# A two-layer diffusion backbone: the up products of its four FFNs in seven block products, with the norm applied ahead of them

## The chip, the cores and the metric

The kernel runs on one core of one Trainium2 chip. The metric is the device time of an execution in microseconds. The kernel before takes 2856.15 us, the median of three runs (2855.18, 2856.15 and 2861.4 us).

## The reference: what is computed

Two layers work on 512 latent tokens and 256 context tokens, 1024 features each, in float32. A layer is a half-step FFN, a token mixer (a convolution, a gated linear attention and a softmax attention side by side between one input and one output projection), and a second half-step FFN. The last FFN has latent tokens only.

```
def pre(x, mod, j, g):
    return rms_norm(x, g) * (1 + mod[:, :, 3 * j + 1]) + mod[:, :, 3 * j]

def half_ffn(x, mod, j, g, w1, w2):
    gu = pre(x, mod, j, g) @ w1          # w1: 1024 x 5632
    a, u = jnp.split(gu, 2, axis=-1)     # gate a and value u, 2816 columns each
    return x + 0.5 * mod[:, :, 3 * j + 2] * ((jax.nn.silu(a) * u) @ w2)
```

`mod` holds nine modulation vectors per layer and kind of token, `silu(c) @ w_ada[i] + b_ada[i]`, with `w_ada[i]` of 1024 x 9216 numbers (a matrix times two vectors: one for the latent tokens, one for the context).

## The kernel before, in words

**Layout.** Features lie on the partitions: the residual x is eight tiles `xt` (K tiles) of 128 features by 768 tokens, the latent ones first. An FFN has 22 column tiles of gate and 22 of value; f counts them, one of each. The four FFNs are called FFN1 to FFN4 here, in the order in which they run.

**Exact pairs.** A float32 operand is kept as a high part, rounded to the type fp32r, and the rest: `split` (L141 to L143) makes the high part on ScalarE (ACT) and the rest on VectorE (DVE). `mm3` (L386 to L393) multiplies two such pairs in three passes, hi by hi (L389), hi by lo (L391) and lo by hi (L393).

**Up.** For each f, `up` (L412 to L428) takes the gate tile and then the value tile. `load_split` (L131 to L139) fetches 512 KB of weights into one of two `raw` buffers and splits them into `whi` (ACT, L137) and `wlo` (DVE, L138), three buffers each. Then come eight K tiles by three passes by two chunks of tokens: 386 and 384 columns in FFN1 to FFN3, 256 and 258 in FFN4. `evac` multiplies the sum by 1/rms from PSUM (DVE, L465) and applies Silu or Identity (ACT, L468); gate and value are multiplied (DVE, L423) and split into `gh` and `gl` (L142, L143).

**The norm comes after.** `Scale.feed` (L355) writes x times the gain as a pair `sh`, `sl` (L362 on ACT, L363 on DVE), which needs no statistics, so that the first products can begin while squares are still being summed (L260 on ACT, L263 on GpSimd, POOL). Two more columns carry the shift vectors through the same products. In FFN1 a class `Head` starts the first tiles while the shifts are still being computed.

**Down.** Two f make a round. After the ups of a round come the down products of the round before, eight output tiles by 512 and 256 tokens; each is added to `xt` by DVE (`add_gated`, L399).

**The modulation vectors.** Vectors 0 and 1 of layer 0 are products on TensorE at the start. The other fourteen are filled in beside the FFNs by `ada` (L183): it loads 256 KB tiles `adaw`, ACT scales each by one number per partition (L195, one operation for each kind of token), DVE adds (L197), and one product per half with ones sums over the partitions (L206). An up is followed by 8 such steps in FFN1, 3 or 4 in FFN2 and FFN3, none in FFN4. The loads rotate through six slots of a group called d.

**What sets the order.** The program text gives the order, and each engine works through its own list; all loads are issued by one queue, SP, in that order too. A load that waits for its buffer holds up those behind it.

Some lines, of `up` and of `ada`:

```
            for t in (f, FT + f)[len(uv):]:
                w = load_split(w1_d[l, i, t])
                p = bigt("up")
                for k in range(KT):
                    mm_up([p[:, p0 + t0:p0 + t0 + n] for t0, n in cols], w, k, cols)
...
                r = slot(tags, "adaw", (P, 512))
                nc.sync.dma_start(out=r, in_=wada_d[l, m, k, :, half * 512:(half + 1) * 512])
                for v in range(nv):
                    t = acc[v] if k == 0 else slot("F", "adat", (P, 512))
                    nc.scalar.activation(out=t, in_=r, func=AF.Copy, scale=sc[:, k, v:v + 1])
                    if k:
                        nc.vector.tensor_tensor(out=acc[v], in0=acc[v], in1=t, op=ALU.add)
```

## Time and profile before

| | |
|---|---|
| runs (three) | 2855.18, 2856.15, 2861.4 us; median 2856.15 |
| profiled execution: span | 2857.3 us; nothing is reported outside the span |
| mean granted TensorE clock | 0.987 of full speed |
| TensorE (PE) busy | 2781.7 us, 97% |
| PE weight loads (PEld, beside PE) | 2541.2 us, 89% |
| DVE busy | 1768.5 us, 62% |
| ACT busy | 1200.8 us, 42% |
| POOL busy | 136.4 us, 5% |
| FFN1, FFN2, FFN3, FFN4 (from the first to the last of their products) | about 62 to 636, 1030 to 1590, 1592 to 2160, 2480 to 2857 us |

The table shares the span among engines that work side by side, so it says who is nearly always busy, and not what a piece of work costs. A matmul's own duration contains the filling and draining of the array, which the next one overlaps: what a matmul costs is the distance between the starts of two neighbours. Names such as `up<-sh,whi` are output and inputs, `128x386` is partitions by elements, x2 joins two like instructions.

### The profile page before, as it was taken

How to read it: one execution, taken by the hardware profiler on the slowest of the kernel's cores; microseconds unless marked ns; L12 is line 12 of the kernel's file. 1: busy time of each engine (PE TensorE's matmuls, PEld its weight loads, DVE VectorE, ACT ScalarE, POOL GpSimd, SP SyncE). 2: the span in 40 equal slices, each digit the busy share in tenths (PEclk: the TensorE clock that was granted, in tenths of full speed). 3: DMA queues.
4: the chain of work that ended last, by engine and by line, in shares of the span. 5: the costliest groups of instructions: out<-in, count | busy, mean ns of one | idle time of the engine just before them, and what ended most of it. 6: DMA issues, size and time to landing. Idle time of an engine off the chain costs nothing. (4 is left out here: it accounts for less than half of the span.)

```text
span 2857.3 us, 42932 instructions
## 1 busy us (share of the span) xinstructions
PE 2781.7 (97%) x17498; PEld 2541.2 (89%) x17498; DVE 1768.5 (62%) x2974; ACT 1200.8 (42%) x1908; POOL 136.4 (5%) x134
## 2 busy tenths in 40 slices
PE   8999999999899999999999999999999989999999
PEld 4999999988687899999999999999997768999998
DVE  4786874464897565566465746454546588555555
ACT  4665662233347454254252523232324447432322
POOL 1000000010300100000000100000001110100000
PEclk9999999999999999999999999999999999999999
DMA  7443441221211243233231313231312131222322
GB/s 255 144 144 129 141 130 60 67 93 58 65 43 27 86 139 101 82 118 107 78 118 56 116 66 111 74 119 60 98 57 84 47 88 28 91 89 95 98 97 89
DMA packets 98501, 267.67 MB, mean 94 GB/s; under 512 B 11520, under 2 KB 11904, under 8 KB 98304
## 3 DMA queue, kind: packets, MB, share of 16 engines
q1 hardware_dynamic: 98304, 264.93, 28.7%
q8 instruction: 137, 2.24, 0.3%
q14 instruction: 60, 0.49, 0.1%
HBM read 249.16 MB, written 7.34 MB: 90 GB/s over the span
## 5 line engine op out<-in xcount | busy, mean ns | idle before, releaser
L137 ACT CAST whi<-raw 128x1024 fp32r<-128x1024 f32 (+1 forms) x314 | 324.6, 1044 | 1110.8 <-PE up L391 524.2
L389 PE MATMUL up<-sh,whi 128*128 128x386 f32 (+1 forms) x2808 | 691.4, 327 | 2.2 <-ACT sh L362 1.2
L391 PE MATMUL up<-sl,whi 128*128 128x386 f32 (+1 forms) x2808 | 687.8, 325 | 4.7 <-DVE sl L363 4.7
L393 PE MATMUL up<-sh,wlo 128*128 128x386 f32 (+1 forms) x2808 | 686.0, 325 | 0.1
L465 DVE TENSOR_TENSOR upv<-up,rb 128x770 f32<-128x770 f32 (+2 forms) x177 | 157.2, 889 | 639.0 <-PE up L393 634.7
L389 PEld LDWEIGHTS up<-sh,whi 128*128 128x128 f32 x2808 | 493.1, 190 | 12.4 <-ACT whi L137 4.2
L391 PEld LDWEIGHTS up<-sl,whi 128*128 128x128 f32 x2808 | 495.9, 190 | 7.5 <-DVE sl L363 7.3
L393 PEld LDWEIGHTS up<-sh,wlo 128*128 128x128 f32 x2808 | 494.1, 190 | 2.1 <-DVE upv L465 1.7
L399 DVE SCALAR_TENSOR_TENSOR xt<-dn,mods,xt 128x512 f32<-128x512 f32 (+1 forms) x616 | 375.2, 632 | 123.0 <-PE dn L393 122.3
L389 PE MATMUL dn<-gh,whi 128*128 128x512 f32 (+1 forms) x1232 | 429.9, 349 | 3.3 <-DVE xt L399 3.2
L138 DVE TENSOR_TENSOR wlo<-raw,whi 128x1024 fp32r<-128x1024 f32 (+1 forms) x314 | 378.6, 1215 | 83.3 <-ACT whi L137 75.1
L391 PE MATMUL dn<-gl,whi 128*128 128x512 f32 (+1 forms) x1232 | 427.7, 347 | 0.0
L393 PE MATMUL dn<-gh,wlo 128*128 128x512 f32 (+1 forms) x1232 | 426.4, 347 | 0.0
L195 ACT ACTIVATE adat<-adaw,sc 128x512 f32<-128x512 f32 x392 | 258.9, 715 | 84.0 <-DVE adacc L197 76.7
L389 PEld LDWEIGHTS dn<-gh,whi 128*128 128x128 f32 x1232 | 232.8, 189 | 45.0 <-ACT whi L137 7.9
L393 PEld LDWEIGHTS dn<-gh,wlo 128*128 128x128 f32 x1232 | 232.9, 189 | 31.2
L391 PEld LDWEIGHTS dn<-gl,whi 128*128 128x128 f32 x1232 | 233.0, 189 | 29.5
L197 DVE TENSOR_TENSOR adacc<-adacc,adat 128x512 f32<-128x512 f32 x392 | 250.4, 684 | 7.9 <-ACT adat L195 6.3
L468 ACT ACTIVATE upv<-upv 128x512 f32<-128x512 f32 (+1 forms) x308 | 179.7, 625 | 33.8 <-DVE upv L465 33.6
L389 PE MATMUL pj<-nh,whi 128*128 128x512 f32 (+1 forms) x328 | 120.5, 371 | 8.5 <-DVE var L572 4.3
L263 POOL TENSOR_TENSOR acc<-acc,sq 128x512 f32<-128x512 f32 (+1 forms) x72 | 76.1, 1057 | 1075.1 <-ACT sq L260 1069.7
L391 PE MATMUL pj<-nl,whi 128*128 128x512 f32 (+1 forms) x328 | 120.9, 369 | 2.4 <-DVE nl L332 2.3
(216 smaller groups left out, 2798.7 us busy)
## 6 DMA issues: line engine op xcount, KB each, us to landing
raw<-in_w_dram SPq DMA_DIRECT2D x264, 512.0 KB, 3.5
adaw<-in_wada_dram SPq DMA_DIRECT2D x288, 256.0 KB, 3.3
raw<-in_wt_dram SPq DMA_DIRECT2D x26, 512.0 KB, 3.4
raw<-in_wo_dram SPq DMA_DIRECT2D x16, 512.0 KB, 3.6
raw<-in_wk_dram SPq DMA_DIRECT2D x8, 416.0 KB, 3.2
xt<-in_xT_dram SPq DMA_DIRECT2D x8, 384.0 KB, 7.9
park<-xt SPq DMA_DIRECT2D x8, 384.0 KB, 2.3
xt<-park SPq DMA_DIRECT2D x8, 384.0 KB, 5.2
```

The source lines that it names most:

```text
L137: nc.scalar.copy(out=hi[:, :n], in_=r[:, :n])
L138: nc.vector.tensor_tensor(out=lo[:, :n], in0=r[:, :n], in1=hi[:, :n].bitcast(F32), op=ALU.subtract)
L195: nc.scalar.activation(out=t, in_=r, func=AF.Copy, scale=sc[:, k, v:v + 1])
L197: nc.vector.tensor_tensor(out=acc[v], in0=acc[v], in1=t, op=ALU.add)
L263: eng.tensor_tensor(out=self.acc[:, t0:t0 + n], in0=self.acc[:, t0:t0 + n], in1=s[:, :n], op=ALU.add)
L389: nc.tensor.matmul(out=o, lhsT=w[0], rhs=m[0][:, t0:t0 + n], start=first, stop=False)
L391: nc.tensor.matmul(out=o, lhsT=w[0], rhs=m[1][:, t0:t0 + n], start=False, stop=False)
L393: nc.tensor.matmul(out=o, lhsT=w[1], rhs=m[0][:, t0:t0 + n], start=False, stop=last)
L399: nc.vector.scalar_tensor_tensor(out=x, in0=o[:, :n], scalar=mods[l][:, v, mod * KT + d:mod * KT + d + 1], in1=x, op0=ALU.mult, op1=ALU.add)
L465: nc.vector.tensor_tensor(out=a[:, t0:t0 + n], in0=p[:, c0:c0 + n], in1=rb[:, t0:t0 + n], op=ALU.mult)
L468: nc.scalar.activation(out=a[:, c], in_=a[:, c], func=AF.Silu if t == f else AF.Identity, bias=a[:, NX + v:NX + v + 1])
```

## The change

**Up products.** The eight K tiles are taken as two halves of four, the tokens as two halves (384 and 384, or 256 and 256 in FFN4), and gate and value of one f as the two blocks of columns. Of a 2 by 2 block product the seven-product form needs seven block products in place of eight: each is 4 K tiles by three passes by one half of the tokens. Its operands are sums and differences of blocks, of the weights (made by POOL in place in the raw tiles, L448 and L449, then split anew) and of the activations (made once per FFN by a class `Combos` in place of `Scale`, on DVE and POOL). The results are joined by sums on DVE and one on POOL (L484).

**The norm ahead of them.** `Combos` needs the finished 1/rms of a half of the tokens before it can make that half's operands. The first two of the seven products use the first half only: for f = 0 to 4 (`HEADS`) they are issued while the second half is being made, and these five gate tiles are loaded twice.

**What is moved with it.** Of the additions for the modulation vectors, DVE now scales and adds the latent one in a single operation (L187); ACT scales the tile in place for the other (L191) and POOL adds it (L193). The tiles `adaw` lie in two slots of group m in place of six of group d. Each half vector is summed and transposed on its own: 144 transposes in place of 72. Steps per up are 7, 5, 4 and 0. Down products come between the two ups of a round in place of behind both. Buffers: `raw` 3, `whi` and `wlo` 4, group E 9 slots. Shift columns, `Scale`, `Head` and the vector start under way are gone; the last round of FFN2 ends by halves of 384 tokens.

```diff
-SLOTS = {"a": 4, "b": 4, "c": 2, "d": 6, "A": 8, "E": 5, "F": 4, "v": 1, "q": 2, "m": 2}
+SLOTS = {"a": 4, "b": 4, "c": 2, "d": 6, "A": 8, "E": 9, "v": 1, "q": 2, "m": 2}
...
+HEADS = 5
+RAW = 3
+RING = 4
...
-                r = slot(tags, "adaw", (P, 512))
+                r = slot("m", "adaw", (P, 512))
                 nc.sync.dma_start(out=r, in_=wada_d[l, m, k, :, half * 512:(half + 1) * 512])
...
+                    nc.vector.scalar_tensor_tensor(out=acc[0], in0=r, scalar=sc[:, k, 0:1], in1=acc[0],
+                                                   op0=ALU.mult, op1=ALU.add)
+                if nv > 1:
+                    t = r if k else acc[1]
+                    nc.scalar.activation(out=t, in_=r, func=AF.Copy, scale=sc[:, k, 1:2])
                     if k:
-                        nc.vector.tensor_tensor(out=acc[v], in0=acc[v], in1=t, op=ALU.add)
+                        nc.gpsimd.tensor_tensor(out=acc[1], in0=acc[1], in1=t, op=ALU.add)
...
+        def build(self, h):
+            nh = self.nh
+            rb = self.spread(self.half(h))
+            yield
+            for p in range(4):
+                a = self.normed(p, h, rb)
+                if h == 0:
+                    self.h0.append(a)
+                    self.pair("xb", a, self.TAGS["b"], ("11", "21"))
+                else:
...
+                    nc.vector.tensor_tensor(out=t13[:, 0], in0=a[:, 0], in1=self.h0[p][:, 0], op=ALU.subtract)
+                    nc.gpsimd.tensor_tensor(out=t24[:, 0], in0=a[:, 1], in1=t13[:, 0], op=ALU.subtract)
+                    nc.vector.tensor_tensor(out=t13[:, 1], in0=a[:, 1], in1=a[:, 0], op=ALU.subtract)
+                    nc.gpsimd.tensor_tensor(out=t24[:, 1], in0=self.h0[p][:, 1], in1=t24[:, 0], op=ALU.subtract)
...
+                    split(b[:, 0], b[:, 1], a[:, 1])
...
+                    self.pair("xt", t13, self.TAGS["13"], ("T1", "T3"))
+                    self.pair("xt", t24, self.TAGS["24"], ("T2", "T4"))
...
+        def prod(o, w, c0, b, start, stop):
+            for p in range(4):
+                ws = slice(c0 + p * P, c0 + (p + 1) * P)
+                hi, lo = b[p]
+                nc.tensor.matmul(out=o, lhsT=w[0][:, ws], rhs=hi, start=start and p == 0, stop=False,
...
+        def up(f, e):
+            ra = load(w1_d[l, i, f])
+            ru = load(w1_d[l, i, FT + f])
+            w1 = wsplit(ra) if e is None else None
+            s1t = wp.tile([P, 512], F32, tag="s1t", name="s1t", bufs=1)
+            lo, hi = slice(0, 512), slice(512, 1024)
+            sub = lambda out, a, b: nc.gpsimd.tensor_tensor(out=out, in0=a, in1=b, op=ALU.subtract)
+            nc.gpsimd.tensor_tensor(out=s1t, in0=ru[:, lo], in1=ru[:, hi], op=ALU.add)
+            sub(ru[:, lo], ra[:, lo], ru[:, lo])
+            sub(ra[:, lo], s1t, ra[:, lo])
+            sub(ra[:, hi], ra[:, hi], ra[:, lo])
+            w24 = wsplit(ra)
+            w5 = [wp.tile([P, 512], F32R, tag=f"w5{n}", name=f"w5{n}", bufs=1) for n in "hl"]
+            split(w5[0], w5[1], s1t)
+            w34 = wsplit(ru)
...
+                prod(oa, w1, 0, x["11"], True, True)
+                nc.scalar.copy(out=s1, in_=oa)
+            prod(ob, w24, 0, x["T2"], True, True)
+            add(u[:, 0], ob, s1)
...
+                prod(oa, w1, 512, x["21"], False, True)
+                nc.scalar.activation(out=sa0, in_=oa, func=AF.Silu)
+            prod(oc, w5, 0, x["T1"], True, True)
+            nc.scalar.copy(out=z[:, 1], in_=oc)
+            prod(od, w34, 0, x["T3"], True, True)
+            add(u[:, 1], od, u[:, 0])
+            prod(oc, w24, 512, x["22"], False, True)
+            add(y[:, 1], oc, u[:, 0])
+            nc.scalar.activation(out=y[:, 1], in_=y[:, 1], func=AF.Silu)
+            prod(od, w34, 512, x["T4"], False, True)
+            nc.gpsimd.tensor_tensor(out=z[:, 1], in0=u[:, 1], in1=z[:, 1], op=ALU.add)
+            add(z[:, 0], od, u[:, 0])
+            mul = lambda out, a, b: nc.vector.tensor_tensor(out=out, in0=a, in1=b, op=ALU.mult)
+            mul(z[:, 0], sa0, z[:, 0])
+            mul(z[:, 1], y[:, 1], z[:, 1])
...
+        head = {}
+        for f in range(HEADS):
+            head[f] = up_head(f)
+            advance(cb.pending)
+        advance(cb.pending, KT)
+        g = {}
         for c in range(FT // 2):
             for q in range(2):
+                if q == 1 and 0 < c < FT // 2 - 1:
+                    down(c - 1, (g[2 * c - 2], g[2 * c - 1]), False)
+                g[2 * c + q] = up(2 * c + q, head.pop(2 * c + q, None))
+                advance(fill, per_up)
```

TensorE, one K tile of an up in FFN1, before: each pass covers both chunks of tokens with one tile of weights (`whi`), K tile after K tile up to the eighth.

```order
L389 MATMUL up_3888<-sh0_157,whi_3884 128x386
L389 MATMUL up_3888<-sh0_157,whi_3884 128x384
L391 MATMUL up_3888<-sl0_165,whi_3884 128x386
L391 MATMUL up_3888<-sl0_165,whi_3884 128x384
L393 MATMUL up_3888<-sh0_157,wlo_3885 128x386
L393 MATMUL up_3888<-sh0_157,wlo_3885 128x384
```

The same place after the change: the product of the first four K tiles of one half of the tokens (`xbh`, `xbl`) is at its end with four K tiles, and its operands are the normed activations.

```order
L421 MATMUL up_2153<-xbh_306,whi_2132 128x384
L423 MATMUL up_2153<-xbl_307,whi_2132 128x384
L424 MATMUL up_2153<-xbh_306,wlo_2133 128x384
L421 MATMUL up_2153<-xbh_318,whi_2132 128x384
L423 MATMUL up_2153<-xbl_319,whi_2132 128x384
L424 MATMUL up_2153<-xbh_318,wlo_2133 128x384
```

An up of a column pair f was 96 such matmuls (16 K tiles of two weight tiles by three by two) and is now 84 (seven products by four by three).

DVE beside the down products of a round of FFN1, before: two additions for the modulation vectors (`adacc`, L197) between the additions to `xt`, each of scaled tiles `adat` that ACT has left.

```order
L197 TENSOR_TENSOR adacc_1629<-adacc_1629,adat_1950 128x512
L197 TENSOR_TENSOR adacc_1953<-adacc_1953,adat_1961 128x512
L399 SCALAR_TENSOR_TENSOR xt5_197<-dn_1766,mods0_78,xt5_197 128x512
L399 SCALAR_TENSOR_TENSOR xt5_197<-dn_1774,mods0_78,xt5_197 128x256
L197 TENSOR_TENSOR adacc_1954<-adacc_1954,adat_1964 128x512
```

After: one operation per tile, straight from the loaded tile `adaw`, which must therefore be read here before ACT and POOL can go on with it.

```order
L407 SCALAR_TENSOR_TENSOR xt6_182<-dn_2096,mods0_78,xt6_182 128x512
L407 SCALAR_TENSOR_TENSOR xt6_182<-dn_2104,mods0_78,xt6_182 128x256
L187 SCALAR_TENSOR_TENSOR adacc_1967<-adaw_2268,sc_82,adacc_1967 128x512
L407 SCALAR_TENSOR_TENSOR xt7_184<-dn_2112,mods0_78,xt7_184 128x512
L407 SCALAR_TENSOR_TENSOR xt7_184<-dn_2120,mods0_78,xt7_184 128x256
L133 TENSOR_TENSOR wlo_2150<-raw_2130,whi_2149 128x1024
```

POOL in the same round after the change (it had nothing there before): the vectors' additions (L193), the four combinations of weights (L448, L449) and the sum that ends an up (L484) share one list.

```order
L193 TENSOR_TENSOR adacc_1968<-adacc_1968,adaw_2258 128x512
L449 TENSOR_TENSOR s1t_2311<-raw_2305 128x512
L448 TENSOR_TENSOR raw_2305<-raw_2303,raw_2305 128x512
L193 TENSOR_TENSOR adacc_1968<-adacc_1968,adaw_2263 128x512
L193 TENSOR_TENSOR adacc_1968<-adacc_1968,adaw_2268 128x512
L193 TENSOR_TENSOR adacc_1968<-adacc_1968,adaw_2273 128x512
L448 TENSOR_TENSOR raw_2303<-s1t_2311,raw_2303 128x512
L448 TENSOR_TENSOR raw_2303<-raw_2303 128x512
L484 TENSOR_TENSOR upz_2158<-upu_2156,upz_2158 128x384
```

Over the whole kernel POOL goes from 77 to 616 operations, DVE from 2526 to 3177; up matmuls go from 8496 (72 of them the short ones of the shifts in `Head`) to 7392, 5544 of 384 columns and 1848 of 256.

## Rows read from the trace of the kernel before

**Rows 1.** The page, busy us (share of the span) of each engine, x instructions.

```profile
PE 2781.7 (97%) x17498; PEld 2541.2 (89%) x17498; DVE 1768.5 (62%) x2974; ACT 1200.8 (42%) x1908; POOL 136.4 (5%) x134
```

**Rows 2.** Windows: span; busy us of PE, PEld, DVE, ACT, POOL; clock, DMA, GB/s.

```profile
0.00:70.00 70.00, 57.06 (x241) 33.55 (x242) 29.45 (x88) 28.89 (x60) 13.99 (x16) 0.93 0.71 255
100.00:380.00 280.00, 280.00 (x1594) 262.95 (x1593) 209.64 (x312) 169.35 (x252) 0.00 (x0) 1.00 0.43 139
1575.00:1600.00 25.00, 21.99 (x111) 19.03 (x110) 24.90 (x41) 18.90 (x37) 13.75 (x12) 0.86 0.17 60
2483.00:2853.00 370.00, 370.00 (x2614) 347.50 (x2613) 197.41 (x246) 107.17 (x130) 0.00 (x0) 1.00 0.28 93
```

**Rows 3.** Timeline, up products of FFN1 and FFN4: start us, us, engine, line.

```profile
307.31 0.52 PE L389 MATMUL up<-sh,whi 128*128 128x386 f32 x2
307.67 0.52 PE L391 MATMUL up<-sl,whi 128*128 128x386 f32 x2
308.02 0.51 PE L393 MATMUL up<-sh,wlo 128*128 128x386 f32 x2
...
2650.20 0.40 PE L391 MATMUL up<-sl,whi 128*128 128x256 f32 x2
...
2652.12 0.28 PE L389 MATMUL up<-sh,whi 128*128 128x256 f32 x1
```

**Rows 4.** Timeline, down products and transposes of FFN1.

```profile
335.21 0.60 PE L167 MATMUL adapt<-glb,adasb 128*128 128x128 f32 x4
335.57 0.47 PE L389 MATMUL dn<-gh,whi 128*128 128x512 f32 x1
...
336.57 0.39 PE L391 MATMUL dn<-gl,whi 128*128 128x512 f32 x1
336.80 0.40 PE L393 MATMUL dn<-gh,wlo 128*128 128x512 f32 x1
```

**Rows 5.** Timeline of the start: first vector's products, first up product.

```profile
6.16 12.67 PE L229 MATMUL adaps<-adaw,spad 128*32 128x512 f32 x32 [6.16 <-DMA adaw<-in_wada_dram]
...
21.17 0.84 PE L389 MATMUL up<-sh,whi 128*128 128x386 f32 x2 [1.21 <-ACT sh L362]
```

**Rows 6.** Groups by form: busy us, mean ns | idle before, releaser.

```profile
L138 DVE TENSOR_TENSOR wlo<-raw,whi 128x1024 fp32r<-128x1024 f32 x306 | 370.4, 1220 | 56.0 <-ACT whi L137 50.7
...
L195 ACT ACTIVATE adat<-adaw,sc 128x512 f32<-128x512 f32 x392 | 258.9, 715 | 84.0 <-DVE adacc L197 76.7 <-DMA adaw<-in_wada_dram 3.6 <-ACT whi L137 1.9
...
L263 POOL TENSOR_TENSOR acc<-acc,sq 128x512 f32<-128x512 f32 x30 | 40.0, 1334 | 197.5 <-ACT sq L260 193.6 <-DVE nrm L328 3.4
...
L328 DVE SCALAR_TENSOR_TENSOR nrm<-xt,gs,st 128x512 f32<-128x512 f32 x16 | 11.0, 739 | 4.7 <-PE st L291 4.7
```

**Rows 7.** DMA issues of 200 to 300 us: KB each, median us to landing.

```profile
adaw<-in_wada_dram SPq DMA_DIRECT2D x30, 256.0 KB, 3.0
raw<-in_w_dram SPq DMA_DIRECT2D x12, 512.0 KB, 3.5
```

**Rows 8.** Waits of the DMA queue: us in total, times, longest us.

```profile
SPq L192 <- ACT adat L195: 255.5, 191, 5.0
```

**Rows 9.** Timeline at 32 to 36 us, POOL and DVE side by side.

```profile
32.30 1.30 POOL L263 TENSOR_TENSOR acc<-acc,sq 128x512 f32<-128x512 f32 x1 [1.26 <-ACT sq L260]
33.67 1.59 POOL L263 TENSOR_TENSOR acc<-acc,sq 128x512 f32<-128x512 f32 x1
35.34 1.35 POOL L263 TENSOR_TENSOR acc<-acc,sq 128x512 f32<-128x512 f32 x1
...
32.30 1.84 DVE L363 SCALAR_TENSOR_TENSOR sl<-xt,gs,sh 128x512 fp32r<-128x512 f32 x1
...
35.47 1.77 DVE L363 SCALAR_TENSOR_TENSOR sl<-xt,gs,sh 128x512 fp32r<-128x512 f32 x1
```

More of the change, by code (lines that the diff above doesn't have):

```diff
@@ L176, in ada_out @@
             if m % 3 == 1:
[L177 to L179 removed]
+                e = (m // 3) * KT + 4 * half
+                nc.vector.scalar_tensor_tensor(out=gs[l][:, v, e:e + 4], in0=d, scalar=1.0,
+                                               in1=cst[l][:, O_GN + e:O_GN + e + 4], op0=ALU.add, op1=ALU.mult)
@@ new lines, in ada @@
+                if nv > 1:
+                    t = r if k else acc[1]
+                    nc.scalar.activation(out=t, in_=r, func=AF.Copy, scale=sc[:, k, 1:2])
+                    if k:
+                        nc.gpsimd.tensor_tensor(out=acc[1], in0=acc[1], in1=t, op=ALU.add)
+                yield
+            ps = smlt("adaps", tag="ao")
+            for v in range(nv):
+                nc.tensor.matmul(out=ps[32 * v:32 * v + 32, :], lhsT=one32, rhs=acc[v], start=True, stop=True)
+            ada_out(l, m, half, nv, ps, 32 * nv, lambda v: 32 * v)
@@ L1137, in backbone_kernel @@
-    head = Head()
-    for k in range(KT):
-        for seg in [SEGX, SEGC]:
-            nm.feed(seg, k)
-    for seg in [SEGX, SEGC]:
+    advance(first)
+    cb = Combos(0, 0, T // 2)
+    for k in range(KT):
+        xt[k] = slot("A", f"xt{k}")
+        nc.sync.dma_start(out=xt[k], in_=xT_d[:, k, :])
+    advance(first, 2)
+    for h in range(2):
         for k in range(KT):
-            nm.square(seg, k)
+            cb.feed(h, k)
     nc.sync.dma_start(out=glb[:, P:G_ONE], in_=glb_d[:, P:G_ONE])
@@ L1162, in backbone_kernel @@
         advance(fill, 1000)
-        nm = mix(l, nxt, last, g, lambda: shifted(Scale(l, 2, o)), half if last else both)
-        g, o = o, g
+        cb = mix(l, nxt, last, "1", lambda: Combos(l, 2, NX // 2 if last else T // 2),
+                 [(0, NX // 2), (NX // 2, NX // 2)] if last else halves)
         if not last:
-            fill = chain(*[ada(1, m, "d" + o) for m in range(5)])
+            fill = chain(*[ada(1, m) for m in range(5)])
             lazy = []
```

444 lines of the change are left out of this document (166 added, 278 removed).

## The prediction

> **What bounds the kernel now.** I read the page's engine line first: TensorE is busy 97% of the span, and no other engine is above 62% [rows 1]. A share averages stages, so the windows come next [rows 2]. The reader is to see PE busy for all of 280 us in FFN1 (the stage with the most work for DVE, 209.64 us) and for all of 370 us in FFN4, at full clock. Only the start and the seam between FFN2 and FFN3 show gaps: 57.06 of 70 us at a clock of 0.93, 21.99 of 25 us at 0.86. So inside an FFN every matmul taken out is worth its full price until something else becomes late, and the seams hold little that could be won. The timeline gives the price. Between the starts at 307.31 and 308.02 us lie four matmuls of 386 columns, 0.1775 us each; between 2650.20 and 2652.12 us lie sixteen of 256, 0.12 us each [rows 3]. A down matmul of 512 columns is 0.23 us from start to start [rows 4]; of 256 I take the same 0.12.
>
> **What is removed.** One up of a pair f has 84 matmuls in place of 96. FFN1 to FFN3 have 66 f: 66 x 12 x 0.1775 = 140 us. FFN4 has 22: 22 x 12 x 0.12 = 32 us. The order of the program fixes these counts, so that the change does not shorten PE's list is no case. Shift columns and short head matmuls go too, under 2 us, which I leave out. Sum so far: -172 us. The price holds if weight loads still hide: PEld is 262.95 of 280 us today, one load per matmul before and after, so I add nothing.
>
> **Small additions on PE.** 72 more transposes at 0.09 us (four between 335.21 and 335.57) [rows 4]: +6.5 us. Loading a gate tile of f = 0 to 4 twice costs PE nothing, since 20 loads of 3.5 us landing [rows 7] lie beside products; if that cover is gone they are part of the start and the seams below.
>
> **Start, +20 us.** Today the first product starts at 21.17 us, because unnormed tiles suffice [rows 5]. Now all eight x tiles, both modulation vectors, sums and 1/rms come first, and the first FFN weights stand in SP's list behind 32 vector tiles, x and constants: 13.2 MB. The first 16 vector tiles, 4.19 MB, took 12.67 us [rows 5]; at that pace 13.2 MB take 40 us, and with 2.6 us before and some 4 of landing and splitting the first product starts near 47 us. Today by 92 us PE has done about 41 us of its work at full pace less what the start lost, and I estimate 25 by then after it, since heads (21 us) and the build of the second half do not quite meet. Bounds: 10 if the build keeps up, 35 if every operand is waited for.
>
> **Seams, +17, +13, +17 us** (mixer to FFN2, FFN2 to FFN3, mixer to FFN4). The first half's 1/rms is hidden: some 8 us of sums, square roots and splits lie beside the other half's down or output products. The second half's is not. From the first half's end DVE has, by the price of a scaled tile and of a split [rows 6] scaled to 384 and 768 columns, 2.45 us per K-tile pair for the first half and 5.45 for the second, four of each, 32 us; eight weight splits of 1.22, 10 us; and I put 10 us of standing still behind POOL (below). That is 52 us against 33 us of PE work that is ready (five heads of 24 x 0.1775, 21 us, and 12 us of the other half). The last K-tile pair can overlap products, so PE stands some 15 us, and a clock of 0.86 as at today's seam [rows 2] takes 2 or 3 more. FFN3's seam has a longer tail of down products (13), FFN4's shorter heads and shorter operands (17). Bounds: 5 and 25 each.
>
> **FFN1, +40 us.** This is the choice that matters. Vector tiles now have two slots in place of six. A slot is free again when the tile has landed (3.0 us [rows 7]), DVE has added it (0.74, by its like operation with a scalar), ACT scaled it (0.715) and POOL added it (1.27 to 1.33) [rows 6], with half a microsecond for taking turns: a lap of 6.5 us for two tiles. A round has 12.4 tiles, so 6.2 laps, 40 us, and 1.56 ends of half vectors at 3 us: 45 us. PE needs 84 x 2 x 0.1775 + 48 x (0.23 + 0.12) = 46.7 us for a round. On average it fits; but the tiles are spaced by program order: beside the down products two tiles fall on 4.2 us of PE work, while their lap takes 6.5. Down products wait on DVE's list, in which the addition of the next tile stands ahead of the addition that frees their PSUM buffer. I count 2.3 us late twice in a round, nine rounds: 40 us. SP already waits for these slots today, 255.5 us in 191 waits [rows 8], and PE loses nothing by it: six slots absorb it. Bounds: 5 (buffers absorb it again) and 124 (below).
>
> **FFN2 +8, FFN3 +3, FFN4 +8 us.** Fewer tiles, or none. What remains is a chain ahead of every up: cast of the gate tile, four combinations on POOL, cast and split of the sum tile, 8 to 10 us against 11.5 us of lead. Bounds: 0 and 20 each.
>
> **The sum**, against the profiled 2857.3 us: -172 + 6.5 + 20 + 47 + 40 + 19 = -39.5, so 2817.8; the median of the runs lies 1.15 us lower, and I forecast **2817 us**.
>
> **DVE and POOL, rows and rule.** Both work on SBUF at once at 32 to 36 us today [rows 9]. They take turns: DVE's first operation ends at 34.14, 0.54 us after POOL's first (33.60); POOL's second ends at 35.26, 1.12 later; DVE's third at 37.24, 0.55 after POOL's third. So a turn of 512 elements is 0.55 us for DVE and 1.12 for POOL, and recorded durations of either hold the other's turn. Per f in FFN1 POOL has 10.2 turns (4 combinations, one sum, 5.4 vector additions), 11.4 us, and DVE's own list is 19.1 us, of which 12.2 read two operands from SBUF. In turns, 0.55 over 0.74 of those 12.2 us is 9.1, and with POOL's 11.4 the two need 20.5 us of an f's 23.4 us: both fit, so my sum has no term for it in FFN1.
>
> The Trainium skill, page "SBUF — State Buffer", section "SBUF: two separate sides", says that a GpSimd operation and a VectorE operation with two SBUF inputs exclude each other for the whole instruction and that the loser blocks fully. The turns above agree that nothing is shared. By that rule with whole recorded lengths as prices, 12.2 and 13.6 us would need 25.8 us, 2.4 more than PE, 43 us over FFN1's 18 f. It speaks against giving POOL this work.
>
> **Rivals.**
> - **A, it is all hidden.** Buffers of four weight tiles and PSUM absorb the uneven slots, as six slots do today. Then FFNs cost 10 in place of 59 and seams 35 in place of 67 with the start: 2817 - 49 - 32 = 2736 us. For it: PE had no gap in 280 us with DVE at 75% [rows 2]. Against it: one list on POOL now stands between the loads and the products. Chance 0.20.
> - **B, two slots bound FFN1: slower.** If waits in POOL's and DVE's lists stretch a lap to 9 us (a tile that arrives just behind a weight combination waits for that one and its inputs), a round is 6.2 x 9 + 4.7 = 60.5 us, 13.8 over PE's: nine rounds 124 us in FFN1, and 27 in FFN2 by the same lap. 2817 - 48 + 151 = **2920 us**. It decides from a lap of 8.2 us, where FFN1 alone gives back what is left of the gain. Against it: the rows' own lengths sum to 6. Chance 0.14.
> - **C, DVE stands behind POOL.** If three quarters of POOL's turns fall on DVE, an f of FFN1 takes DVE 19.1 + 8.6 = 27.7 us, 4.3 over PE, 77 us in 18 f; FFN2, with fewer tiles, 25.1, so 31 us; and the seams 6 each. 2817 - 48 + 77 + 31 + 18 = 2895 us. Against it: the turns in rows 9. Chance 0.14.
>
> **How the numbers follow.** Forecast 0.52, A 0.20, B 0.14, C 0.14. The forecast's own range is 2760 to 2850, from the bounds of its terms, not all at one end at once. B's top and A's lowest end are left out, less than 2 in 10: 2735 to 2900 us. No change that a measurement can tell is 0.2%, 5.7 us around 2856. Slower: B and nearly all of C less the milder forms of both, 0.25 in all; same, the edge of the forecast's and C's tails, 0.05; faster 0.70.
>
> **What the profile would show.** Right: 7392 up matmuls at 0.177 and 0.12 us; a round of FFN1 near 51 us, with PE's waits in the down products and SP waiting for POOL at the vector tiles; PE idle 15 to 20 us in each seam; first product near 47 us; POOL busy some 870 us. A: rounds of 47 us. B: rounds of 60 us, SP waiting on POOL almost always, and DVE idle meanwhile. C: DVE busy through the rounds, its two-operand rows well above today's. The forecast is wrong at its root if PE's price per matmul rises, or if seams stay under 5 us or go over 30.

## The result, and the profile after

The changed kernel takes 3204.3 us (median of four runs, 3199.32 to 3208.17), against 2856.95 us for the kernel before beside it. The ratio is 1.121, with a 95% interval of 1.120 to 1.123: 347 us slower, where 2817 us was forecast and 2900 us was the top of the range.

The page of the changed kernel, engines and slices of the span, which answers to [rows 1]:

```profile
PE 2828.5 (88%) x16490; PEld 2449.4 (76%) x16490; DVE 2144.4 (67%) x3406; ACT 1198.3 (37%) x1936; POOL 1020.3 (32%) x774
...
PE   7798889999896988888989879999999878888888
...
POOL 2645544411210035443442242222221200433332
PEclk8799999999998998999999989999999989999999
```

TensorE issues 1008 matmuls fewer and still has more busy time, with a share of 88% in place of 97%. POOL is the new tenant: 1020 us, 32%. The clock is 0.948 on the mean, where it was 0.987. Its two levels here are full speed (2.4 GHz) and half (1.2), so the core spent 2 x 0.052 x 3206 = 333 us at half speed, against 74 us before.

Windows of the changed kernel, one for each stage in the order FFN1, mixer, FFN2, FFN3, mixer, FFN4 (columns as in [rows 2]):

```profile
51.00:741.00 690.00, 602.25 (x3046) 517.51 (x3047) 494.70 (x678) 269.98 (x404) 320.25 (x228) 0.94 0.30 101
741.00:1163.00 422.00, 373.21 (x2755) 319.61 (x2753) 260.59 (x605) 177.78 (x342) 47.08 (x46) 0.95 0.17 52
1163.00:1818.00 655.00, 578.32 (x3010) 512.11 (x3010) 460.75 (x630) 241.83 (x361) 272.51 (x199) 0.96 0.27 89
1818.00:2424.00 606.00, 559.39 (x2995) 499.13 (x2994) 418.65 (x602) 191.31 (x288) 172.38 (x133) 0.97 0.28 93
2424.00:2759.00 335.00, 292.09 (x2203) 246.61 (x2203) 210.28 (x468) 149.83 (x274) 38.47 (x36) 0.92 0.20 59
2759.00:3201.00 442.00, 384.74 (x2382) 341.24 (x2381) 288.67 (x395) 152.77 (x246) 157.50 (x118) 0.94 0.24 82
```

No stage has PE busy throughout. Before, the windows of FFN1 and FFN4, from their first up matmul to their last down matmul, were these:

```profile
21.00:630.00 609.00, 601.12 (x3372) 553.87 (x3373) 405.78 (x622) 305.10 (x469) 25.18 (x25) 0.99 0.37 123
2475.00:2853.00 378.00, 377.65 (x2676) 354.82 (x2675) 203.41 (x264) 111.02 (x137) 0.99 (x1) 1.00 0.28 92
```

From the first up matmul of an FFN (in FFN3 from the end of FFN2) to the last down matmul, and what lies between, in us:

| | start | FFN1 | mixer | FFN2 | FFN3 | mixer | FFN4 |
|---|---|---|---|---|---|---|---|
| before | 21 | 609 | 381 | 580 | 573 | 310 | 378 |
| after | 51 | 690 | 422 | 655 | 606 | 335 | 442 |
| difference | +30 | +81 | +41 | +75 | +33 | +25 | +64 |

A round of two pairs (mean of the seven distances between the first down products of eight steady rounds) is 60.8, 58.1, 51.5 and 38.4 us in FFN1 to FFN4; before it was 52.1, 51.7, 51.4 and 34.0. By the prices of [rows 3] and [rows 4] its matmuls now need 46.7 us, and 31.2 in FFN4. Even the two mixers, whose own work the change does not touch, are longer.

At full clock the price of a matmul did not move. The timeline of PE in FFN4 (start us, us, engine, line) shows 0.12 us from start to start, as in [rows 3], then a hole, and behind the hole 0.21 us:

```profile
2986.76 0.28 PE L421 MATMUL up<-xth,w5h 128*128 128x256 f32 x1
2986.88 0.28 PE L423 MATMUL up<-xtl,w5h 128*128 128x256 f32 x1
2987.00 0.28 PE L424 MATMUL up<-xth,w5l 128*128 128x256 f32 x1
2990.10 0.39 PE L421 MATMUL up<-xbh,whi 128*128 128x256 f32 x1 [2.82 <-ACT upe L475]
...
2990.60 0.42 PE L421 MATMUL up<-xth,whi 128*128 128x256 f32 x1
2990.81 0.42 PE L423 MATMUL up<-xtl,whi 128*128 128x256 f32 x1
2991.03 0.41 PE L424 MATMUL up<-xth,wlo 128*128 128x256 f32 x1
```

The window there has a granted clock of 0.50, the lower of the two levels:

```profile
2990.60:2993.80 3.20, 3.20 (x17) 3.20 (x16) 1.42 (x3) 0.23 (x1) 0.00 (x0) 0.50 0.53 164
```

So this hole costs its own length and then 3 us of matmuls at nearly twice their price. Over the whole kernel PE was busy in 286 us of its half-speed time, against 65 before. At 0.213 in place of 0.12 us a matmul these 221 us more are some 100 us of the loss; this is an estimate from the rows above.

The timelines of ACT and of POOL around the hole say why it is there:

```profile
2982.16 0.37 ACT L470 COPY upe<-up 128x256 f32<-128x256 f32 x1 [0.30 <-PE up L424]
2988.72 1.04 ACT L132 CAST whi<-raw 128x1024 fp32r<-128x1024 f32 x1 [6.19 <-POOL raw L448]
2989.67 0.38 ACT L475 ACTIVATE upe<-up 128x256 f32<-128x256 f32 x1
```

```profile
2981.75 2.00 POOL L449 TENSOR_TENSOR s1t<-raw 128x512 f32<-128x512 f32 x1 [5.64 <-DMA raw<-in_w_dram]
2983.83 2.14 POOL L448 TENSOR_TENSOR raw<-raw 128x512 f32<-128x512 f32 x1
2986.05 1.30 POOL L448 TENSOR_TENSOR raw<-s1t,raw 128x512 f32<-128x512 f32 x1
2987.43 1.26 POOL L448 TENSOR_TENSOR raw<-raw 128x512 f32<-128x512 f32 x1
```

PE waits for a Silu of 0.38 us that frees its PSUM tile (L475). The sums for that Silu were ready, but it stands in ACT's list behind the cast of the next weights (L132), and the cast waits 6.19 us for POOL's fourth combination, 1.3 to 2.1 us each. One late weight tile stops work that has nothing to do with it.

DVE's own rows in FFN1 (52 to 690 us, groups by form: busy us, mean ns | idle before) are the second sign:

```profile
L133 DVE TENSOR_TENSOR wlo<-raw,whi 128x1024 fp32r<-128x1024 f32 x85 | 119.4, 1410 | 41.0 <-ACT whi L132 40.8
...
L187 DVE SCALAR_TENSOR_TENSOR adacc<-adaw,sc,adacc 128x512 f32<-128x512 f32 x98 | 97.8, 998 | 31.4 <-DMA adaw<-in_wada_dram 30.8
...
L467 DVE TENSOR_TENSOR upy<-up,upu 128x384 f32<-128x384 f32 x21 | 11.6, 554 | 26.9 <-PE up L424 26.9
```

The weight split took 1220 ns before [rows 6] and takes 1410. The vector's addition takes 998 ns, where a like operation took 739. Both read two operands from SBUF. The sum that reads PSUM (L467) is not stretched: 554 ns here, and 555 in a run below where POOL does nothing in the FFNs.

### The profile page after: what moved, and what is told of

It reads as the page before. It is cut to its first block, busy times and chain, and to the rows that moved or that the text cites. A ratio compares the mean times of both kernels' runs of the same rounds, so it can differ in the third digit from the quotient of the medians.

```text
span 3206.4 us, 42772 instructions
## 1 busy us (share of the span) xinstructions
PE 2828.5 (88%) x16490; PEld 2449.4 (76%) x16490; DVE 2144.4 (67%) x3406; ACT 1198.3 (37%) x1936; POOL 1020.3 (32%) x774
## 5 line engine op out<-in xcount | busy, mean ns | idle before, releaser
L132 ACT CAST whi<-raw 128x1024 fp32r<-128x1024 f32 (+1 forms) x402 | 416.2, 1044 | 1123.3 <-PE up L423 353.1
L396 PE MATMUL dn<-gh,whi 128*128 128x512 f32 (+2 forms) x1232 | 439.4, 357 | 35.5 <-DVE xt L407 22.4
L407 DVE SCALAR_TENSOR_TENSOR xt<-dn,mods,xt 128x512 f32<-128x512 f32 (+3 forms) x624 | 374.2, 625 | 117.9 <-PE dn L400 116.3
L400 PE MATMUL dn<-gh,wlo 128*128 128x512 f32 (+2 forms) x1232 | 428.2, 350 | 8.5 <-DVE wlo L133 8.5
L398 PE MATMUL dn<-gl,whi 128*128 128x512 f32 (+2 forms) x1232 | 431.0, 350 | 4.1 <-DVE gl L141 4.1
L421 PE MATMUL up<-xth,whi 128*128 128x384 f32 (+1 forms) x1056 | 362.9, 344 | 48.1 <-ACT whi L132 11.0
L423 PE MATMUL up<-xtl,whi 128*128 128x384 f32 (+1 forms) x1056 | 349.9, 331 | 4.9 <-DVE xtl L141 4.8
L424 PE MATMUL up<-xth,wlo 128*128 128x384 f32 (+1 forms) x1056 | 348.3, 331 | 5.2 <-DVE wlo L133 5.2
L193 POOL TENSOR_TENSOR adacc<-adacc,adaw 128x512 f32<-128x512 f32 x168 | 250.0, 1488 | 310.4 <-ACT adaw L191 291.3
L421 PE MATMUL up<-xbh,whi 128*128 128x384 f32 (+1 forms) x704 | 249.0, 358 | 69.7 <-ACT upe L475 34.8
L187 DVE SCALAR_TENSOR_TENSOR adacc<-adaw,sc,adacc 128x512 f32<-128x512 f32 x224 | 227.4, 1015 | 76.1 <-DMA adaw<-in_wada_dram 74.8
L449 POOL TENSOR_TENSOR s1t<-raw 128x512 f32<-128x512 f32 x88 | 126.3, 1436 | 450.5 <-DMA raw<-in_w_dram 425.2
L448 POOL TENSOR_TENSOR raw<-raw 128x512 f32<-128x512 f32 x176 | 255.8, 1454 | 12.7
```

The lines of the kernel that those rows point to most:

```text
L132: nc.scalar.copy(out=hi[:, :n], in_=r[:, :n])
L187: nc.vector.scalar_tensor_tensor(out=acc[0], in0=r, scalar=sc[:, k, 0:1], in1=acc[0], op0=ALU.mult, op1=ALU.add)
L193: nc.gpsimd.tensor_tensor(out=acc[1], in0=acc[1], in1=t, op=ALU.add)
L396: nc.tensor.matmul(out=o, lhsT=w[0], rhs=m[0][:, t0:t0 + n], start=first, stop=False)
L398: nc.tensor.matmul(out=o, lhsT=w[0], rhs=m[1][:, t0:t0 + n], start=False, stop=False)
L400: nc.tensor.matmul(out=o, lhsT=w[1], rhs=m[0][:, t0:t0 + n], start=False, stop=last)
```

## The experiments

Unless said otherwise a run is one timed execution and one profile, which separates differences over some 10 us. They fall into four groups, and then make a ladder.

### The mixers: who claims a buffer first

DVE's 120 taps of the first mixer's convolution (L905 before, L928 after) were at 699 to 852 us before, beside the linear attention. In the changed kernel all of them lie in the softmax attention. One line's instructions before (first row) and after, minimum, median and maximum ns, first and last start:

```profile
L905 DVE SCALAR_TENSOR_TENSOR cacc<-hc,cst,cacc x60: 468/485/1586, 698.7 to 852.4; 128x256 f32<-128x256 f32 x60
L928 DVE SCALAR_TENSOR_TENSOR cacc<-hx,cst,cacc x60: 675/742/1834, 940.5 to 1047.7; 128x512 f32<-128x512 f32 x60
L928 DVE SCALAR_TENSOR_TENSOR cacc<-hc,cst,cacc x60: 473/476/480, 941.2 to 1048.4; 128x256 f32<-128x256 f32 x60
```

The change merged the group F of short-lived tiles into E, where the convolution's sums `cacc` live. A tile is claimed at its first write, which for `cacc` stands late in the program, behind the claims of all the short-lived ones.

```diff
             cv.append(slot("E", "cacc"))
+            nc.gpsimd.memset(cv[c][:, 0:1], 0.0)
```

> The only edit: the two tiles of the convolution's sum are written once (one column) where the program allocates them, ahead of the short-lived tiles of the mixer, which share their group since the change. Theory 'allocation order': in the changed kernel the convolution's taps stand behind the last of those tiles and fall into the attention, where DVE then makes TensorE wait; with the tiles claimed early the taps go back beside the linear attention. First mixer 422 -> about 382 us, second 335 -> about 311, whole kernel 3204 -> about 3140. Rival 'seam': the mixers are longer because of the norm at their end; then both stay within 8 us of 422 and 335, and the total above 3185.

Measured: 3132.27 us, 72 us less. The first mixer is 381.4 us and the second 308.6, which is what they were before; the taps start again early in the mixer:

```profile
L929 DVE SCALAR_TENSOR_TENSOR cacc<-hc,cst,cacc x60: 470/484/1575, 801.1 to 941.2; 128x256 f32<-128x256 f32 x60
```

The theory holds: its numbers are met within 8 us. The norm at the mixers' end adds nothing to them that shows.

### Is it the seven products, the norm, or the vectors?

Run e2 keeps the change and puts the eight block products back.

```diff
-            w24 = wsplit(ra)
...
-            w34 = wsplit(ru)
+            wa, wu = wsplit(ra), wsplit(ru)
...
+                prod(oa, wa, 0, x["11"], True, False)
+                prod(oa, wa, 512, x["21"], False, True)
...
+            prod(od, wu, 0, x["12"], True, False)
+            prod(od, wu, 512, x["22"], False, True)
```

> All of the change but its seven products: norm ahead, halves of tokens, heads, two slots for the vector tiles, additions on POOL, buffers; the up products are the eight block products again, and no combinations of weights or operands are made. Theory 'weight chain' (the four POOL combinations and three more splits per pair set the rounds): rounds of the last FFN go from 39 to 33.6 us and of the third from 51.2 to 50.6 or less (what 96 products need), first and second FFN to 52 or less; total 2980 to 3020. Rival 'vector slots' (two slots and POOL's additions set the first two FFNs): these stay at 56 to 59 us a round, total above 3080. Rival 'norm ahead' (the seams cost most): rounds fall, but the four starts still cost 30 us or more each over before, total above 3050.

Measured: 2996.65 us, 208 less, with rounds of 57.0, 54.0, 51.7 and 33.9 us. The last two FFNs are back at the rounds of the kernel before (51.4 and 34.0). So the seven products cost 208 us more than eight in this kernel, where their count alone is worth 172 less: some 380 us go into feeding them. The first two FFNs, whose rounds lie above the 52 expected, keep a smaller second cause.

Run e3 keeps the seven products and leaves out the four POOL combinations of each pair's weights.

```diff
-            nc.gpsimd.tensor_tensor(out=s1t, in0=ru[:, lo], in1=ru[:, hi], op=ALU.add)
-            sub(ru[:, lo], ra[:, lo], ru[:, lo])
-            sub(ra[:, lo], s1t, ra[:, lo])
-            sub(ra[:, hi], ra[:, hi], ra[:, lo])
```

> Leaves out the four POOL operations per pair that combine the weights (the same seven products, splits and buffers, on raw weights). Theory 'weight chain through POOL': rounds of the last FFN 39 -> 32 us or less (PE needs 30.9), third 51 -> 47.5, first 58.6 -> 52, second 56 -> 50; total 3204 -> 2980 to 3040. Rival 'vector slots': last two FFNs gain under 3 us a round, first two stay above 55; total above 3120. Rival 'splits and PE order' (what stalls are the casts and splits, seven sets in place of four, and the order of products): rounds of the last FFN stay above 36.

Measured: 3033.11 us, 171 less; rounds 55.8, 53.9, 49.6 and 33.6. FFN4 falls from 442 to 388.5 us. The combinations on POOL are about half of the loss, and not all of it.

Run e4 leaves out POOL's other new work, the context vector's additions.

```diff
-                    if k:
-                        nc.gpsimd.tensor_tensor(out=acc[1], in0=acc[1], in1=t, op=ALU.add)
```

> Leaves out the additions of the context vector on POOL (168 operations); loads, DVE's additions and ACT's scaling stay. Theory 'vector slots and POOL': first FFN's rounds 58.6 -> 49 us or less, second 56 -> 49; total 3204 -> 3020 to 3060. Rival 'weight chain': first FFN's rounds lose 4 us or less, second's 3 or less, the last two nothing; total above 3130.

Measured: 3098.73 us, 106 less, nearly all in FFN1 (629.0) and FFN2 (618.1). This lies between the two theories: either kind of POOL work costs. In e11 below, where POOL has no combinations left, the additions still cost 96 us, so the two kinds nearly add.

### POOL: the work, the slots, or the engine?

Run e5 does the combinations on DVE.

```diff
-            sub = lambda out, a, b: nc.gpsimd.tensor_tensor(out=out, in0=a, in1=b, op=ALU.subtract)
-            nc.gpsimd.tensor_tensor(out=s1t, in0=ru[:, lo], in1=ru[:, hi], op=ALU.add)
+            sub = lambda out, a, b: nc.vector.tensor_tensor(out=out, in0=a, in1=b, op=ALU.subtract)
+            nc.vector.tensor_tensor(out=s1t, in0=ru[:, lo], in1=ru[:, hi], op=ALU.add)
```

> The four combinations of weights per pair on DVE in place of POOL, all else as changed. Theory 'POOL is slow in the chain' (1.44 us each there, waited for by the casts behind it): rounds of the last FFN 38.4 -> 35 us, third 51.5 -> 49.5, first 60.8 -> 56 (POOL is left to the vectors); total 3204 -> 3070 to 3120. Rival 'it is the length of the chain and the buffers it holds, not the engine': last FFN's rounds stay within 1.5 us; first two get longer, since DVE is at 70% there; total 3180 to 3260.

Measured: 3059.39 us, 145 less. Doing the combinations on DVE costs only 26 us more than not doing them at all (e3), although DVE has 352 operations more. FFN4's rounds fall to 33.4 us. It is the engine.

Runs e6 and e7 ask whether a fourth buffer for loads would have done as well.

```diff
-RAW = 3
+RAW = 4
```

> Four buffers for loaded weights in place of three (8 slots in group E in place of 9 and two copies of small tiles in place of four make the room; the next run is the same without the fourth). Theory 'loads come late' (a raw tile is held from its load to the end of POOL's work and the split after it, so the next load waits): against the next run the rounds of the last FFN fall by 3 us or more, the total by 60 or more. Rival 'the split tiles are what is short' (four of each for eight per round): under 15 us in all.

> Control for the run before it: 8 slots in group E and two copies of small tiles, three raw tiles. If group E is not short: within 20 us of 3204. If it is: longer by 30 or more, most of it in the starts of the FFNs, where the operands are made.

Measured: 3197.24 and 3214.01 us. FFN4 gains 29 us (rounds 38.2 to 34.9), but the other FFNs lose 5 to 8 us each. Late loads are part of FFN4's loss only.

Run e8 sets PE's list in the order of the program text.

```diff
+        with tc.manual_schedule(engines={mybir.EngineType.PE}):
```

> TensorE's list in the steady part of each FFN in the order of the program text (whole products, down products between the two ups) in place of the order that the compiler interleaves. Theory 'a product set too early holds up those behind it' (3 of 12 matmuls of the next up's first product stand inside the up before and wait for its PSUM tile): last FFN's rounds 38.4 -> 35, total 3204 -> 3110 to 3150. Rival 'weights are late whatever the order': rounds within 1 us, total within 30. Rival 'interleaving hides waits': slower by 40 or more.

Measured: 3510.25 us, 306 slower. The interleaved order, for all its holes, hides more waits than it makes.

Run e9 puts everything but the context vector on DVE (combinations, the differences `t24`, the sum L484) and has e1's edit as well.

> Combinations of weights, the two differences per pair of operands and the sum at an up's end all on DVE, and the convolution's sums claimed early: POOL keeps only the context vectors and squares. Theory: the two causes add (3204 - 145 - 72 = 2987), and the operands at each start come out some 8 us earlier since no step of their chain is on POOL: 2945 to 2965. Rival 'DVE is full at the starts': the starts (first product to first down product) stay at 78, 79, 75 and 53 us or grow, total 2980 to 3010.

Measured: 2976.73 us. The causes add (2987 by the sum); against e5 the starts of the FFNs moved by -3, -5, +1 and -6 us, so the rival was nearer there.

Run e10 is e9 with the fourth raw tile, as in e6.

> The run before it with four raw tiles (8 slots in group E, two copies of small tiles). If loads still come late in the last FFN, its 388 us with combinations on DVE fall by 15 us or more and the total by 10 or more; if the chain without POOL is short enough for three, within 8 us of the run before.

Measured: 2969.27 us, 7 less, none of it in FFN4 (386 against 378). Without POOL in the chain three raw tiles are enough.

Run e11 is e9 without the context vector's additions (left out, as in e4).

> The run e9 without the additions of the context vector on POOL (left out, 168 operations). What the two slots and POOL's additions still cost by my recorded estimate is 2.3 us twice a round in the first FFN, 40 us, and 8 in the second: the total falls by 35 to 60, all of it in the first two FFNs. Rival: with POOL free of weights its additions no longer wait in line, and the total falls by under 15.

Measured: 2880.56 us, 96 less, above what was expected of it: 55 in FFN1, 31 in FFN2 and 5 in the first mixer. POOL with this work alone, busy 152 us in FFN1 of e9, still costs that much. Two theories were left, and e12 and e13 part them. Run e12 (the first edit) does the additions on DVE; run e13 (the second) leaves POOL as many operations, with a constant in place of the loaded tile, so that no slot waits for POOL (the context vector's sums are left out there, and POOL multiplies by the constant).

```diff
-                        nc.gpsimd.tensor_tensor(out=acc[1], in0=acc[1], in1=t, op=ALU.add)
+                        nc.vector.tensor_tensor(out=acc[1], in0=acc[1], in1=t, op=ALU.add)
```

```diff
-                        nc.gpsimd.tensor_tensor(out=acc[1], in0=acc[1], in1=t, op=ALU.add)
+                        nc.gpsimd.tensor_tensor(out=acc[1], in0=acc[1], in1=cos, op=ALU.mult)
```

> Run e9 with the context vector's additions on DVE too (168 of 0.55 to 0.69 us, some 60 us in the first FFN, 40 in the second): POOL has nothing left in the FFNs. If what the additions cost on POOL was POOL (its length in the slots' lap, or keeping DVE out), the total falls from 2977 to 2890 to 2925; if two slots are too few whatever engine adds, or DVE is full, it stays above 2950.

> Run e9 with as many POOL operations of the same size as the context vector's additions, but on a constant in place of the loaded tile (so that vector's sums are left out): no slot waits for POOL any more, DVE and POOL run side by side as before it. Theory 'lap of two slots': the first two FFNs fall to those of e11, total 2880 to 2905. Rival 'POOL keeps DVE out of SBUF': DVE's two-operand rows stay as long as in e9 (1274 ns for 128x1024) and the total stays at 2950 or above.

Measured: 2903.52 us for e12 and 2997.60 for e13, which is 21 slower than e9 itself. Taking POOL out of the slots' lap gains nothing; taking the work off POOL gains 73 us.

The cleanest pair is e11 and e13. PE, DVE and ACT work through the same lists in both, instruction for instruction; e13 has POOL's 168 operations besides, on tiles that no DVE operation writes, and takes 117 us more. FFN1 of e11 and of e13, as windows:

```profile
52.40:653.70 601.30, 568.36 (x3050) 500.61 (x3051) 484.97 (x796) 269.89 (x403) 12.54 (x12) 0.97 0.34 117
50.30:716.50 666.20, 590.11 (x3050) 516.12 (x3051) 558.33 (x795) 271.11 (x403) 172.11 (x111) 0.94 0.31 105
```

DVE is busy 73 us longer for the same operations, and PE's waits for DVE in this stage sum to 62 us in place of 17. FFN1 of e13, groups by form:

```profile
L193 POOL TENSOR_TENSOR adacc<-adacc,glb 128x512 f32<-128x512 f32 x98 | 159.2, 1625 | 371.3 <-ACT adacc L191 347.6 <-PE adapt L164 17.1
...
L133 DVE TENSOR_TENSOR wlo<-raw,whi 128x1024 fp32r<-128x1024 f32 x90 | 118.5, 1322 | 28.2 <-ACT whi L132 27.5
...
L187 DVE SCALAR_TENSOR_TENSOR adacc<-adaw,sc,adacc 128x512 f32<-128x512 f32 x98 | 97.2, 992 | 7.3 <-DMA adaw<-in_wada_dram 7.0
```

The same of e12, in which POOL has nothing in FFN1 but squares:

```profile
L133 DVE TENSOR_TENSOR wlo<-raw,whi 128x1024 fp32r<-128x1024 f32 x90 | 109.5, 1219 | 14.4 <-ACT whi L132 14.1
...
L187 DVE SCALAR_TENSOR_TENSOR adacc<-adaw,sc,adacc 128x512 f32<-128x512 f32 x98 | 73.0, 745 | 2.8 <-DMA adaw<-in_wada_dram 2.5
L193 DVE TENSOR_TENSOR adacc<-adacc,adaw 128x512 f32<-128x512 f32 x98 | 67.0, 684 | 2.5 <-ACT adaw L191 2.1
...
L467 DVE TENSOR_TENSOR upy<-up,upu 128x384 f32<-128x384 f32 x22 | 12.2, 555 | 11.0 <-PE up L424 10.8
```

In e13 these operations of POOL and DVE share no data, and still DVE's operations with two operands from SBUF grow from 745 to 992 ns and from 1219 to 1322. The mean hides two kinds. Over all of e13, 170 of the 224 rows of L187 meet no operation of POOL and take 734 to 755 ns; the 54 that meet one take 1516 ns on the mean. The timelines of POOL and of DVE show how:

```profile
229.10 1.43 POOL L193 TENSOR_TENSOR adacc<-adacc,glb 128x512 f32<-128x512 f32 x1 [35.09 <-ACT adacc L191]
230.60 1.61 POOL L193 TENSOR_TENSOR adacc<-adacc,glb 128x512 f32<-128x512 f32 x1
232.30 1.50 POOL L193 TENSOR_TENSOR adacc<-adacc,glb 128x512 f32<-128x512 f32 x1
...
229.30 1.78 DVE L187 SCALAR_TENSOR_TENSOR adacc<-adaw,sc,adacc 128x512 f32<-128x512 f32 x1
231.00 0.55 DVE L467 TENSOR_TENSOR upu<-up,upu 128x384 f32<-128x384 f32 x1
231.58 1.05 DVE L484 TENSOR_TENSOR upz<-upu,upz 128x384 f32<-128x384 f32 x1
232.56 1.79 DVE L187 SCALAR_TENSOR_TENSOR adacc<-adaw,sc,adacc 128x512 f32<-128x512 f32 x1
```

POOL's first row ends at 230.53 and DVE's first at 231.08, 0.55 us later; POOL's third ends at 233.80 and DVE's last at 234.35, again 0.55 later. That is the turn of [rows 9]: DVE's work on two SBUF operands is done behind POOL's operation. The row that reads PSUM (L467) passes beside POOL's second row in its usual 0.55 us.

An addition costs DVE 684 ns when it does it itself. On POOL the 98 additions of FFN1 stretch this one line of DVE by 98 x 0.247 = 24 us and the splits by 9 (e12 to e13), in places that the program order does not choose, and PE's list waits behind them. The lap of two slots is not the main cause: in e12 SP still waits 332 us for DVE to free them, and the kernel is 73 us faster than e9. That it has no share in e9 is not shown, since e13's POOL, which waits for no tile, works in bursts and stretches DVE's rows more than e9's (992 against 835 ns).

### What is left of the seven products

Run e14 leaves out both, additions (as e11) and combinations (as e3).

> Run e11 without the combinations of weights too (left out, 352 operations of DVE): what is left of the seven products is splits, joins, operands and order. Theory 'DVE at 78% sets the rounds': third FFN's rounds 50 -> 47.5, last's 32.9 -> 31.3, total 2880 -> 2815 or less. Rival 'four split tiles and the order of products': rounds stay within 1 us of e11, total above 2855.

Measured: 2875.86 us, 5 less than e11; rounds of FFN3 and FFN4 49.5 and 33.6 us. So DVE's load does not set the rounds; the rival held.

Runs e15 and e16 (e14 without the split of the sum tile, too) ask for the split tiles, of which a round takes eight pairs and has four.

```diff
-RING = 4
+RING = 5
```

> Control for the next run: run e14 (no combinations, no additions of the context vector) with the split of the sum tile left out too (its product uses a block that is split anyway), 8 slots in group E and two copies of small tiles, which makes room. Four split tiles. Third FFN's rounds 49 to 50, last FFN's 33 to 34 us, as in e14.

> The run before it with five pairs of split tiles in place of four. Theory 'split tiles are short' (a round takes eight of them, and the cast waits until a product has released one): third FFN's rounds 49.5 -> 47.5 or less, last's 33.5 -> 31.5, 60 us or more in all. Rival 'the order of products and the joins in PSUM': rounds within 0.7 us, total within 20.

Measured: 2897.53 and 2862.83 us: 35 less by one pair more. FFN2 and FFN3 gain 10 and 11 us (rounds 51.1 to 49.5, 50.0 to 48.2), FFN4 5. Little more than half of what was expected, so the split tiles are a part of the distance to 46.7 and 31.2 us. The rest, the order of products and the joins in PSUM among it, was not taken apart.

Run e17 is the eight products on the footing of e12, in four timed executions.

> The eight block products with the norm ahead (as e2), with the context vector's additions on DVE and the convolution's sums claimed early: what e12 is with seven. By the parts seen so far: 2997 - 72 for the mixer, and 20 to 45 for POOL's 168 additions: 2880 to 2905. If seven products pay on an equal footing, this is slower than e12's 2903.5 by the 172 us less what the rounds give back; if they give all of it back, within 20 of it or faster.

Measured: 2882.72 us, 1.008 times the kernel before (1.0064 to 1.0097). That is 21 us less than e12, which has seven. Rounds of e17 and e12 are 53.9 and 52.5, 52.4 and 50.9, 51.7 and 49.9, 33.9 and 32.8 us: the seven products gain 1.1 to 1.8 us a round out of the 4.3 (3 in FFN4) that their count is worth. They lose it at both ends of an FFN. From the first product to the first down product e17 takes 67, 62, 66 and 42 us, e12 73, 70, 72 and 49, though e12 has 252 to 264 up matmuls there and e17 336. And from the down products of the ninth round to the end e17 takes 108, 108, 111 and 67 us, e12 121, 113, 118 and 74, with the 12 to 36 up matmuls more that PE's list has moved there.

### The ladder

Each step is a kernel that ran, with nothing left out; the order of the steps is one of several. From step to step the engines' lists differ in places, as those of e11 and e13 do not, so a step is the price of an edit with the order that comes with it:

| step | us | adds |
|---|---|---|
| before | 2857 | |
| norm ahead, halves, new starts, eight products (e17) | 2883 | +26 |
| seven products in place of eight (e12) | 2904 | +21 |
| context vector's additions on POOL (e9) | 2977 | +73 |
| combinations, differences and an up's last sum on POOL (e1) | 3132 | +156 |
| convolution's sums claimed late (the change) | 3204 | +72 |

Two thirds of the loss, 229 us, come with POOL. No rung beats the kernel before.

## Why the prediction was wrong

**The price of what is removed** was right at full clock: 0.1775 and 0.12 us a matmul. It was not where the loss came from.

**"DVE and POOL, rows and rule"** is the step that failed: "both fit, so my sum has no term for it in FFN1". It read the turns of [rows 9] rightly, 0.55 us behind POOL's end as in e13, but took them as the whole price of sharing and compared totals per pair, 20.5 against 23.4 us. The engines' lists did fit on the average (DVE 495 of 690 us). But each is a list in order: a stretched DVE operation or a late POOL combination holds up whatever stands behind it. The term put at nothing is worth 117 us from e11 to e13, where POOL's additions touch no data of DVE, and all of POOL's new work comes to 229 us in the ladder. The Trainium skill, page "SBUF — State Buffer", section "SBUF: two separate sides", says that a VectorE operation with two SBUF inputs and a GpSimd operation that reads SBUF exclude each other for the whole instruction. The runs agree: two-operand rows grow (998 against 745 ns), rows that read PSUM do not (554 and 555). By that rule the first FFN alone came to +43 us; the prediction set the rule aside for the turns.

**FFN1 +40, from two slots**, had about the right size for the additions on their own and the wrong mechanism. What e9 pays for them is 41 us in FFN1 and 24 in FFN2 over e12, but with the same two slots in both. Run e13 takes POOL out of the lap and stays slow, so that the size came out is luck.

**FFN2 +8, FFN3 +3, FFN4 +8, "a chain ahead of every up"**: the chain was seen and priced as covered, 8 to 10 us against 11.5 of lead. In FFN4 of the changed kernel (2760 to 3200 us, groups by form) ACT's casts wait 78.5 us for POOL, POOL's combinations wait 138 us for loads, and each combination takes 1.3 to 1.5 us:

```profile
L132 ACT CAST whi<-raw 128x1024 fp32r<-128x1024 f32 x84 | 87.0, 1046 | 196.4 <-POOL raw L448 78.5 <-issue 55.7 <-PE up L423 43.4
L448 POOL TENSOR_TENSOR raw<-raw 128x512 f32<-128x512 f32 x44 | 65.7, 1493 | 3.4
L449 POOL TENSOR_TENSOR s1t<-raw 128x512 f32<-128x512 f32 x22 | 33.6, 1526 | 152.0 <-DMA raw<-in_w_dram 138.0 <-DVE upu L467 9.5 <-DVE w5l L141 4.5
```

FFN4 lost 64 us where 17 for its seam and 8 for this chain were given, and e5 takes 53 of it back by changing the engine.

**Seams +17, +13, +17**: about right without POOL, too low with it. In e12 the first product to the first down product takes 28, 23, 27 and 17 us more in the four FFNs than the 252 to 264 up matmuls of that stretch need (45 to 47 us, 32 in FFN4). Before, with 384 matmuls there, it was some 5 in FFN2 to FFN4, so e12's seams cost some 18, 22 and 13 us; with eight products (e17, 336 matmuls) the stretch is only 2 to 8 over. In the change itself, with POOL, it is 42, 38, 37 and 28: seams of some 33, 33 and 23 us, two of them beyond the 30 that the prediction named as a sign of its being wrong. **The start, +20**, was right at 92 us, where it took stock: 222 long up matmuls had started before and 106 after, 20.6 us of work at 0.1775. The first product came at 51.4 us, though, not 47, and FFN1 went on losing up to its first down product.

**The mixers** had no term at all beside the seam. That F went into E was in the diff, and was read as room. It is also an order of claims, worth 72 us here.

**The split tiles** were not priced: seven products take eight pairs of them per round in place of six.

**The clock** was given 2 to 3 us a seam. Half-speed time grew by some 259 us (333 less 74), some 100 us of the loss by the estimate above, and follows the holes: FFN4 ran at 1.00 in [rows 2] and at 0.94 after; in e17, where PE is busy 97%, the mean clock is 0.987 again. It multiplies the other causes; that it is none of its own is argued from this, since no run changes the clock alone.

**The rivals.** A, all hidden, fell with the result. C had the mechanism, at 2895 us and a chance of 0.14. It charged three quarters of POOL's turns to DVE's list, 8.6 us an f; against the lengths of the same operations in e11, DVE's rows in FFN1 of the change are 81 us longer, 3.7 an f. The loss came all the same, since C left out that the weights' chain passes through POOL, that ACT's list stops behind it, and the mixers. B fell with e13. Its signs were there, a round of 60.8 us and the waits of the DMA queue (us in total, times, longest us), where [rows 8] had ACT:

```profile
SPq L183 <- POOL adacc L193: 525.8, 164, 10.6
```

But in e13 the queue does not wait for POOL there, and the kernel is no faster than e9: a queue that waits is not yet a bound.

## What to carry to other kernels

Fewer matmuls pay only if what feeds them is not the new bound: count, for each product saved, the operations that prepare and join operands, and on whose ordered list they stand. An engine that is idle 95% of the time is not free help when it shares operands' memory with a busy one; a trial with the same operations on unrelated data tells its price without touching dependences. And merging buffer groups changes the order in which tiles are claimed, so look in the order of instructions for work that was early before and is late now.

## What the runs showed of the hardware that was not expected

POOL's addition of 128x512 takes 1290 ns with little beside it (squares of FFN1 in e11), 1509 in the changed kernel and 1625 in e13; DVE does the same in 684. The Trainium skill, page "GPSIMD Engine Reference", section "3.1 Elementwise — side-by-side cycle accounting", has GpSimd 1.96 times slower on a 2048-element addition; the rows here show 1.9 with POOL undisturbed and 2.4 beside DVE. Handing the additions over also cost DVE more time than doing them. In FFN1 DVE is busy 485 us without the 98 additions (e11), 538 when it does them itself (e12) and 558 when POOL does as many beside it (e13). The stage takes 601, 616 and 666 us: what DVE does in its own order hides for the most part, and what POOL makes it wait does not.
